# Issuing the first Q and the first K transfer of an attention kernel in two parts of 16 and 112 partitions

## The chip, the cores and the metric

The kernel runs on one core of a Trainium2 chip. A core has five engines that work side by side: TensorE (PE in the profile; its weight loads are listed as PEld), VectorE (DVE), ScalarE (ACT), GpSimd (POOL) and SyncE (SP), which here only issues transfers. Sixteen DMA engines move data between the chip's large memory (HBM) and the core's on-chip memory (SBUF, 128 partitions). The metric is the device time of one execution in microseconds (us).

## What is computed

For each of 8 x 12 = 96 heads, Q, K and V are 512 x 64 float32 arrays. The reference, cut to its core:

```
Q_norm = Q / (norm(Q, axis=-2) + 1e-10)        # norm over the 512 rows
K_norm = K / (norm(K, axis=-2) + 1e-10)
attn = einsum('bhnd,bhne->bhde', Q_norm, K_norm)       # 64 x 64 for each head
attn = exp(attn - max(attn)); attn = attn / (sum(attn) + 1e-10)
out = einsum('bhnd,bhde->bhne', V, attn)               # 512 x 64 for each head
```

Three inputs of 12.6 MB each are read once and one output of 12.6 MB is written once, so 50.3 MB of data pass through the DMA engines.

## The kernel before

Four heads make a unit `u` (HU = 4; 24 units), two units a step `s` (12 steps), two steps a group `w` (6 groups). A Q or K load of one unit fills 128 partitions with 4,096 bytes each (512 KB): 32 partitions a head, 16 rows of 64 numbers in each. In the middle of the program one load brings both units of a step (1,024 KB).

For every unit VectorE casts Q and K to bf16 side by side (`cast_qk`, line 213). TensorE multiplies this [Q|K] block with itself (`grams`, line 233), which gives the cross products K'Q and, on the diagonal, the squares from which the norms come. VectorE takes the diagonal (`squares`, line 240; `sums`, line 252), ScalarE makes the reciprocal norms (lines 258 and 259), GpSimd or VectorE scales (`scale_k`, line 263), TensorE transposes (`logits`, line 276), ScalarE takes the exponentials (line 282), VectorE normalises (line 291). V is loaded, cast (GpSimd, line 170, or VectorE, line 168), transposed on TensorE (line 302), copied back (line 166 or 168) and multiplied with the normalised matrix (`outs`, line 319). The result is copied from PSUM and stored (`store`, lines 204 to 207). Line 204 stores one result in three pieces of 92, 4 and 32 partitions.

The order of all this is laid down at build time by a planner, the class `Order`: each piece of work names engines with costs, what it comes after, and a rank. The planner plays the program through and hands back the order in which the pieces are emitted. Transfers are pieces of an engine called DMA, with at most `QUEUE = 8` in flight: in the program, too, an issue waits until the transfer eight places before it has landed.

The first four loads are not emitted where the planner has them, but ahead of everything else (the list `ahead`, line 462, and these lines):

```
    for r in range(2):
        load_qk(0, 0, r)
        load_qk(0, 1, r)
```

`load_qk(s, x, r)` loads Q (x = 0) or K (x = 1) of unit `2 * s + r`. For step 0, K goes through ScalarE's queue (line 181) and Q through SyncE's (line 187); all later loads go through SyncE's. The load named `HELD`, the K load of step 1's second unit, first lets VectorE write one number into its tile (line 179), and it and the loads behind it are emitted only after the piece `UNTIL`, the cast of unit 0's K. `UNTIL` and the first casts wait for the first loads to land.

The planner knows nothing of how a load is divided into transfers: its piece for a load is one transfer, before and after the change.

Of the kernel before, what the change touches and what calls it, by code (L numbers as in the profile page):

```python
# [102 lines left out]
def kernel(  # L103
# [7 lines left out]
    nc = tc.nc  # L111
# [15 lines left out]
    Qu = Q.rearrange("b h (p t) d -> (b h p) (t d)", t=T).rearrange("(w r e p) x -> w e p r x", r=2, e=2, p=128)  # L127
    Ku = K.rearrange("b h (p t) d -> (b h p) (t d)", t=T).rearrange("(w r e p) x -> w e p r x", r=2, e=2, p=128)
# [33 lines left out]
    qk32, v32, vb, qkb, gram, scr, kq, n2, r8, kqs, rq, lg, ex, ab, vps, vt, po, so = ({} for _ in range(18))  # L162
# [9 lines left out]
    def load_qk(s, x, r):  # L172

        w, e = divmod(s, 2)
        if s not in qk32:
            qk32[s] = qp.tile([128, 2, 2, T, D], F32, name="qk32")
        if HELD == ("l" + "qk"[x], s, r):

            nc.vector.memset(qk32[s][0:1, x, r, 0, 0:1], 0.0)
        if (s, x) == (0, 1):  # L180
            nc.scalar.dma_start(out=qk32[s][:, x, r].rearrange("p t d -> p (t d)"), in_=Ku[w, e, :, r])
        elif 2 * s + (r or 0) >= WIDE:
            nc.sync.dma_start(out=qk32[s][:, x, r].rearrange("p (m j) d -> p m (j d)", m=2), in_=(Qw, Kw)[x][U - 1])
        elif r is None:
            nc.sync.dma_start(out=qk32[s][:, x].rearrange("p r t d -> p r (t d)"), in_=(Qu, Ku)[x][w, e])
        else:
            nc.sync.dma_start(out=qk32[s][:, x, r].rearrange("p t d -> p (t d)"), in_=(Qu, Ku)[x][w, e, :, r])
# [143 lines left out]
# [3 lines that stand above are left out]
# [50 lines left out]
    for s in range(S):  # L384
        free = [back("cq", 2 * s + r, 2 * NB["qk"], x) for r in range(2) for x in range(2)]
        for r in parts(s):
            at = QK_PACE * (2 * s + (r or 0)) / U
            for x in range(2):
                key = loaded(x, s, r)
                piece(key, {"DMA": X if r is not None else 2 * X}, free, [last], at, load_qk, s, x, r)  # L390
                last = key
    for u in range(U):
        s, r = divmod(u, 2)
# [48 lines left out]
    for s in range(S):  # L442
        for x in range(4):
            i, k = divmod(x, 2)
# [59 lines left out]
```

## Time and profile before

The time before is 128.76 us, the median of three runs (128.62 to 128.79). The profile is of one execution. Its page gives the span from the first to the last instruction, 127.0 us; it does not list a time of that execution's own beside it. The median of the runs is 1.76 us longer than the span.

| | |
|---|---|
| median of three runs | 128.76 us |
| span of the profiled execution | 127.0 us |
| busy: TensorE, VectorE, ScalarE, GpSimd | 77.7, 92.8, 72.5, 36.6 us |
| moved by DMA | 50.64 MB, mean 399 GB/s over the span |
| mean granted TensorE clock | 0.832 |
| share of SyncE's DMA queue q1, of ScalarE's q10 | 96.4%, 2.1% |
| first Q and K issues begin | 0.74 and 0.73 us |
| first cast of Q begins | 5.39 us |
| last computing ends | 115.1 us |

How to read the lines that follow. In the strip of forty slices each digit is the busy share of a slice in tenths, 9 being 90% or more; the DMA row is the mean over the sixteen engines, and the row below gives GB/s. The same strip can be asked for a short window and then has slices of some ten nanoseconds. A packet is what one DMA engine moves at a time; the loads of Q and K use packets of 4,096 bytes, one for each partition. A packet counts in the slice in which it starts, with its whole duration, so a share in a very short window can be over 1. In a timeline a line gives start, duration, engine, source line, operation, tiles and count, and in brackets how long the engine had been idle and what released it; SPq and ACTq are the queues on which transfers are issued.

### The profile page before, as it was taken

The page shows a single profiled execution, that of the slowest core. Times are in us where ns is not written, and L with a number is a line of the kernel's source. Part 1 is how long each engine was busy: PE and PEld are TensorE (multiplying, and loading weights), DVE is VectorE, ACT ScalarE, POOL GpSimd, SP SyncE. Part 2 cuts the span into 40 slices and gives each one's busy share as a digit, 9 for nine tenths or more (in the row PEclk, how much of TensorE's full clock was granted, in tenths as well). Part 3 has the DMA queues.
Part 4 walks back from the last instruction along what each step waited for, and adds up shares of the span by engine and source line. Part 5 has one row for each costly group of instructions (what it writes and reads, how often), then busy time and mean ns, then how long its engine had stood idle before and what let it go on. Part 6 is the DMA issues. An engine that isn't in the chain of part 4 may idle for free.

```text
span 127.0 us, 4887 instructions
## 1 busy us (share of the span) xinstructions
PE 77.7 (61%) x2128; PEld 62.9 (50%) x2128; DVE 92.8 (73%) x141; ACT 72.5 (57%) x220; POOL 36.6 (29%) x40
## 2 busy tenths in 40 slices
PE   0065384894844679858594879566797869680000
PEld 0054372773633568647482668445585748460000
DVE  3354749859899899999885898999999799820000
ACT  4000441569877077786692786794829969972000
POOL 4006307300906903033065212213453361200000
PEclk9999999999998555999958967998559995955555
DMA  4999999999999999999999999999999999999993
GB/s 114 415 434 410 430 410 418 417 437 403 425 426 415 410 419 421 405 415 426 430 410 413 415 421 427 412 419 428 401 413 410 403 402 406 401 405 408 405 366 106
DMA packets 15629, 50.64 MB, mean 399 GB/s; under 512 B 1144, under 2 KB 1656, under 8 KB 14200
## 3 DMA queue, kind: packets, MB, share of 16 engines
q1 hardware_dynamic: 15320, 49.29, 96.4%
q10 hardware_dynamic: 288, 1.05, 2.1%
q8 instruction: 16, 0.26, 0.7%
q14 instruction: 5, 0.04, 0.1%
HBM read 37.75 MB, written 12.58 MB: 396 GB/s over the span
## 4 chain that ended last, share of the span: by engine, by line
DVE 39%; DMA 21%; PE 13%; ACT 11%; issue 4%; POOL 2%; DVEq 0%; SPq 0%; POOLq 0%; ACTq 0%
DMA qk<-in_Q_dram 21%; DVE qkb L213 15%; PE gram L233 9%; DVE scr L240 7%; DVE ab L291 6%; ACT vt L166 4%; DVE vb L168 4%; ACT ex L282 3%; ACT so L166 3%; PE vps L302 3%; DVE n L252 2%; DVE vt L168 2%; DVE so L168 2%; PE po L319 1%; ACT kq L166 1%
## 5 line engine op out<-in xcount | busy, mean ns | idle before, releaser
L233 PE MATMUL gram<-qkb 32*128 32x128 bf16 (+1 forms) x1504 | 35.5, 257 | 23.1 <-DVE qkb L213 9.9
L233 PEld LDWEIGHTS <-qkb 32*128 32x128 bf16 (+1 forms) x1504 | 29.9, 114 | 27.7 <-DVE qkb L213 12.7
L213 DVE CAST qkb<-qk 128x1024 bf16<-128x1024 f32 x48 | 36.4, 780 | 8.5 <-DMA qk<-in_Q_dram 6.9
L170 POOL TENSOR_SCALAR vb<-v 128x1024 bf16<-128x1024 f32 x19 | 21.2, 1129 | 45.5 <-DMA v<-in_V_dram 32.0
L166 ACT COPY so<-po 128x512 f32<-128x512 f32 x45 | 25.0, 593 | 5.2 <-PE po L319 5.0
L166 ACT COPY vt<-vps 128x1024 bf16<-128x1024 bf16 (+1 forms) x18 | 17.8, 989 | 17.4 <-PE vps L302 17.3
L302 PE MATMUL vps<-identb,vb 128*128 128x128 bf16 x192 | 20.2, 262 | 5.8 <-POOL vb L170 3.7
L319 PE MATMUL po<-ab,vt 128*64 128x128 bf16 x384 | 19.3, 242 | 5.2 <-issue 2.7
L263 POOL TENSOR_TENSOR kqs<-kq,r 64x512 f32<-64x512 f32 x12 | 14.0, 1164 | 25.8 <-ACT r L259 13.4
L240 DVE SCALAR_TENSOR_TENSOR scr<-gram,eye 64x512 f32<-64x512 f32 x24 | 16.5, 687 | 4.4 <-PE gram L233 4.1
L302 PEld LDWEIGHTS <-vb 128*128 128x128 bf16 x192 | 14.7, 117 | 10.0 <-POOL vb L170 5.1
L319 PEld LDWEIGHTS <-vt 128*64 128x64 bf16 x384 | 13.8, 121 | 9.2 <-issue 4.6
L282 ACT ACTIVATE ex<-lg,rq 128x64 f32<-128x64 f32 x48 | 14.5, 322 | 2.8 <-PE lg L276 2.7
L166 ACT COPY kq<-gram 64x512 f32<-64x512 f32 x12 | 7.0, 581 | 13.5 <-DVE scr L240 13.4
L291 DVE TENSOR_TENSOR ab<-ex,rinv 64x256 bf16<-64x256 f32 x24 | 13.9, 579 | 0.6
L282 ACT ACTIVATION_READ_ACCUMULATOR ex<-lg,rq 128x1 f32 x48 | 10.2, 213 | 0.0
L168 DVE CAST vb<-v 128x1024 bf16<-128x1024 f32 x5 | 7.6, 1527 | 1.2 <-DMA v<-in_V_dram 1.2
L252 DVE TENSOR_REDUCE n<-scr 128x8 f32<-128x512 f32 x12 | 8.1, 679 | 0.1
L276 PE MATMUL lg<-eye,kqs 64*128 64x64 f32 x48 | 6.4, 259 | 2.6 <-issue 1.5
L168 DVE COPY vt<-vps 128x1024 bf16<-128x1024 bf16 (+1 forms) x8 | 7.9, 1019 | 0.1
L276 PEld LDWEIGHTS lg<-eye,kqs 64*128 64x128 f32 x48 | 4.5, 156 | 4.4 <-issue 2.0
L288 DVE RECIPROCAL rinv<-esum 128x4 f32<-128x4 f32 x12 | 2.1, 171 | 2.8 <-ACT ex L282 2.8
(17 smaller groups left out, 16.0 us busy)
## 6 DMA issues: line engine op xcount, KB each, us to landing
v<-in_V_dram SPq DMA_DIRECT2D x11, 1024.0 KB, 17.1
out_dram<-so SPq DMA_DIRECT2D x22, 512.0 KB, 10.2
qk<-in_Q_dram SPq DMA_DIRECT2D x8, 1024.0 KB, 17.4
qk<-in_K_dram SPq DMA_DIRECT2D x8, 1024.0 KB, 17.1
qk<-in_Q_dram SPq DMA_DIRECT2D x8, 512.0 KB, 12.2
qk<-in_K_dram SPq DMA_DIRECT2D x6, 512.0 KB, 12.5
qk<-in_K_dram ACTq DMA_DIRECT2D x2, 512.0 KB, 7.3
v<-in_V_dram SPq DMA_DIRECT2D x2, 512.0 KB
```

Source lines behind the costliest of these rows:

```text
L166: nc.scalar.copy(o, i)
L168: nc.vector.tensor_copy(o, i)
L170: nc.gpsimd.tensor_scalar(out=o, in0=i, scalar1=1.0, scalar2=0.0, op0=ALU.mult, op1=ALU.add)
L213: nc.vector.tensor_copy(qkb[u][:, :, x * D:(x + 1) * D], qk32[s][:, x, r])
L233: nc.tensor.matmul(gram[s][:, h, r, 0], x, x, start=(t == 0), stop=(t == (T if u < WIDE else J) - 1))
L240: nc.vector.scalar_tensor_tensor(out=scr[s][half], in0=gram[s][half, :, :, 0, half].rearrange("p h r d -> p (h r) d"), scalar=1e-20, in1=e ...
L263: (nc.vector if eng == "DVE" else nc.gpsimd).tensor_tensor(out=kqs[s][HI], in0=kq[s][HI], in1=r8[s][HI, :, None].to_broadcast([D, 2 * HU, ...
L276: nc.tensor.transpose(l[:, h, :], kqs[s][HI, 2 * h:2 * h + 2].rearrange("p r d -> p (r d)"), eye2[HI])
L282: nc.scalar.activation(e[:, h, :], lg[s][:, h, :], AF.Exp, scale=rq[s][:, h:h + 1], accum_out=z[:, h:h + 1])
L291: nc.vector.tensor_tensor(out=a[half, :, half], in0=e[half], in1=ri[half, :, None].to_broadcast([D, HU, D]), op=ALU.mult,)
L302: nc.tensor.transpose(ps[:, c, n, :], vb[w][:, J * c + j].rearrange("p r d -> p (r d)"), identb)
L319: nc.tensor.matmul(po[s, x][e * D:(e + 1) * D, j].rearrange("p r d -> p (r d)"), v, ab[s][:, h, :])
```

## The change

For step 0, both Q and K now go through one branch. The loads of its second unit (r = 1) stay one transfer. The load of the first unit (r = 0) is issued as two transfers, one of partitions 0 to 15 (64 KB) and one of partitions 16 to 127 (448 KB), on the same queue as before: SyncE's for Q, ScalarE's for K. So SyncE issues one transfer more than before and ScalarE one more, and the first cast of each waits for two landings. Nothing else in the program is edited.

```
-        if (s, x) == (0, 1):
-            nc.scalar.dma_start(out=qk32[s][:, x, r].rearrange("p t d -> p (t d)"), in_=Ku[w, e, :, r])
+        if s == 0:
+            o, i = qk32[s][:, x, r].rearrange("p t d -> p (t d)"), (Qu, Ku)[x][w, e, :, r]
+            for rows in (slice(0, 16), slice(16, 128)) if r == 0 else (slice(None),):
+                (nc.sync, nc.scalar)[x].dma_start(out=o[rows], in_=i[rows])
         elif 2 * s + (r or 0) >= WIDE:
```

## The prediction

> **What bounds the kernel now.** I read the strip of forty slices first, then the DMA queues, then the first microseconds as a timeline, then the flow of the DMA engines in short windows at both ends. The strip of the page:
>
> ```profile
> DVE  3354749859899899999885898999999799820000
> DMA  4999999999999999999999999999999999999993
> GB/s 114 415 434 410 430 410 418 417 437 403 425 426 415 410 419 421 405 415 426 430 410 413 415 421 427 412 419 428 401 413 410 403 402 406 401 405 408 405 366 106
> DMA packets 15629, 50.64 MB, mean 399 GB/s; under 512 B 1144, under 2 KB 1656, under 8 KB 14200
> ```
>
> Each slice is 3.17 us. The DMA engines are full in every slice but the first and the last, at about 412 GB/s, while VectorE is free in the last four. The chain of waits gives VectorE 39% and DMA 21%, but it cannot say what a faster VectorE would meet: the engines that move the data have no hole to fill. So the program ends when 50.64 MB have passed, and it can end sooner only if the stream starts sooner, runs faster, or drains more evenly. Windows over the end say the same:
>
> ```profile
> 115.00:116.00 1.00, 0.00 (x0) 0.00 (x0) 0.00 (x0) 0.08 (x1) 0.00 (x0) 0.50 1.06 410
> 116.00:117.00 1.00, 0.00 (x0) 0.00 (x0) 0.00 (x0) 0.00 (x0) 0.00 (x0) 0.50 1.05 406
> 117.00:118.00 1.00, 0.00 (x0) 0.00 (x0) 0.00 (x0) 0.00 (x0) 0.00 (x0) 0.50 1.05 404
> 122.00:123.00 1.00, 0.00 (x0) 0.00 (x0) 0.00 (x0) 0.00 (x0) 0.00 (x0) 0.50 0.92 353
> 124.00:125.00 1.00, 0.00 (x0) 0.00 (x0) 0.00 (x0) 0.00 (x0) 0.00 (x0) 0.50 0.73 258
> ```
>
> The columns are the window, its length, busy time of PE, its weight loads, VectorE, ScalarE and GpSimd, the granted clock, the DMA share and GB/s. All computing is over at 115.1 us, and the stores still run at 400 GB/s for seven microseconds; then engines drop out one after another. Computing therefore has several microseconds of slack at the end, and a stream moved by x moves the end by x.
>
> The change lies at the start, whose timeline reads:
>
> ```profile
> 0.73 0.89 ACTq L181 DMA_DIRECT2D qk<-in_K_dram  x2
> 0.74 0.85 SPq L187 DMA_DIRECT2D qk<-in_Q_dram  x2
> 1.64 0.42 SPq L194 DMA_DIRECT2D v<-in_V_dram  x1
> 1.65 1.28 ACT L338 ACT_TABLE_LOAD   x1 [1.65 <-PEq L488]
> 5.39 1.29 DVE L213 CAST qkb<-qk 128x1024 bf16<-128x1024 f32 x2 [3.44 <-DMA qk<-in_Q_dram]
> ```
>
> Both queues begin to issue at 0.73 us. The DMA view cut to 1.6 to 2.3 us shows what came of it:
>
> ```profile
> GB/s 0 0 0 0 0 0 0 0 702 0 468 468 234 0 234 0 234 0 234 468 0 0 234 234 234 0 234 0 234 234 0 234 0 0 0 0 234 702 234 0
> DMA packets 25, 0.10 MB, mean 146 GB/s; under 512 B 0, under 2 KB 0, under 8 KB 25
> q1 hardware_dynamic: 25, 0.10, 66.8%
> ```
>
> A slice is 17.5 ns, and 234 GB/s is one packet of 4,096 B. The first packets start at 1.74 us, 1.0 us after the issue began, and the next come one by one; the sixteenth, one for each of the 16 engines, starts near 2.03. All are of SP's queue q1, the Q transfer. K's queue q10 has none, although ScalarE issued at the same moment; a view to 2.4 us holds its first five. So K's 128 rows come into the engines about 0.56 us behind Q's 128 rows, as if the rows of one transfer were prepared after those of the other, at some 0.56/128 = 4.4 ns a row (an estimate from these two starts). Windows of the ramp:
>
> ```profile
> 1.80:2.00 0.20, 0.00 (x0) 0.00 (x0) 0.15 (x1) 0.20 (x1) 0.20 (x1) 1.00 1.02 164
> 2.00:2.20 0.20, 0.00 (x0) 0.00 (x0) 0.00 (x0) 0.20 (x1) 0.03 (x1) 1.00 0.54 123
> 2.60:2.80 0.20, 0.00 (x0) 0.00 (x0) 0.00 (x0) 0.20 (x1) 0.00 (x0) 1.00 1.30 287
> 3.40:4.00 0.60, 0.00 (x0) 0.00 (x0) 0.00 (x0) 0.00 (x0) 0.00 (x0) 1.00 1.03 423
> ```
>
> At 412 GB/s the 0.56 us from 1.74 to 2.3 would hold 56 packets, and there were 25: 31 x 4,096 B / 412 GB/s = 0.31 us lost. From 2.3 to 3.3 us the view counts 77 packets where 100 fit: 0.23 us more. After that the stream is full. The whole ramp costs 0.54 us.
>
> **The change part by part.** The sum is made on the profiled execution's span, 127.0 us; the median of the three runs is 128.76, so 1.76 us lie outside the span, and I leave these alone.
>
> *The first transfer gets short.* Q's first issue carries 16 rows in place of 128. The trace has issues of few rows: the three stores of line 204, of 92, 4 and 32 partitions, took 0.26, 0.32 and 0.34 us (minimum, median, maximum), against 0.33 to 0.46 us for undisturbed issues of 128 rows at lines 181 and 187. The first packet should come earlier by that, 0.07 to 0.16 us; I take 0.10. If packets wait until all rows of their transfer are prepared, 112 fewer rows at 4.4 ns bring 0.49 us; if rows are handed over one by one, only the issue counts. The slow trickle between 1.74 and 2.03 speaks for handing over one by one, so I take the 0.10.
>
> *All engines begin together.* Sixteen packets on 16 engines would start within 16 x 4.4 ns = 0.07 us rather than over 0.29, if each engine gets one. K's 16 rows should follow at once, and two packets an engine (0.32 us at 0.159 us each, 4,096 B at a sixteenth of 412 GB/s; 0.8 us at the 0.41 us that the eight packets of the window from 1.8 to 2.0 took on average) keep the engines busy until the 112-row parts are there. Those are issued some 0.33 us behind the first parts. I take 0.20 of the 0.31 us; the bounds are none of it and 0.54, the whole ramp.
>
> *What it adds.* Two more transfers make 32 more 4-byte completion packets. The page has 1,144 such packets; two an engine cost 0.02 us by my estimate, since one-packet transfers of this kind leave no hole at 117 us. One more issue on SP (about 0.4 us) moves the V load from 1.64 to 2.0 and what follows on that queue by as much; the transfers before it hold 2.1 MB, five microseconds of flow, which covers it. One more issue on ScalarE moves the table load from 1.65 to about 2.05; ScalarE's first use is at 12.85, so it costs nothing while 9 us of cover stand. GpSimd's queue is not passed.
>
> *Waits.* There are eight transfers in flight (the planner's QUEUE), and a ninth issue waits for the first landing. With two more in front, the issues at 2.80 (K) and 3.37 us (Q) of the second pair come to be ninth and tenth and wait for the first parts, at worst for the landing of Q's 112 rows, until now 5.4 us. Behind them stand only loads that line 179's memset holds until 6.74 anyway. By then 3.7 MB are issued, which last until 2.3 + 8.9 = 11.2 us: cost nothing. From the eleventh on the eight-back partner is the same as now. The first cast waits for two landings instead of one; if it came 0.5 us later, the next cast, which waits for data until 7.98, would still be met (casts end at 6.68).
>
> Sum: -0.10 - 0.20 + 0.02 = -0.28 us; rounded with the stall of 2.6 to 2.8 us, which may shrink a little too, -0.3: 126.7 us of span, **128.45 us**. Bounds of this case: from about -0.05 (the issue alone, against the added packets) to -0.62 (issue and whole ramp).
>
> [...]
>
> **The rivals.** *Slower: the narrow parts write slowly.* Place: the sixteen packets per engine of the first Q and K. If a transfer of 16 or 112 rows lays several engines' writes on the same partitions, each packet takes longer than 0.159 us. Against it: the line 204 stores of 92, 4 and 32 partitions pass between 116 and 119 us, where the flow stays at 404 to 410 GB/s. But these read SBUF, and the change writes it. For it: packets in the ramp can be slow, 0.30 us on average in the window from 2.6 to 2.8 (share 1.30 x 0.2 us x 16 engines, over 14 packets). At a mean of 0.20 us the price is 16 x 0.041 = 0.66 us, less the 0.28 gained: +0.38, 129.1 us. It decides from 0.177 us a packet, where gain and loss meet.
>
> *No change: the slow start belongs to the first packets, not to the rows.* If the engines' first reads are slow whatever the transfer's size (0.41 us on average), the small part only takes the slow packets upon itself, and what the earlier issue brings is eaten by the second issue's delay. Time: 128.7, give or take 0.1. For it speaks that the DMA share is already 1.02 between 1.8 and 2.0: the engines count as busy, yet move 164 GB/s. The gap of 0.54 between 2.0 and 2.2 speaks against it.
>
> *The gain is lost behind.* If one engine that is late anyway sets the end, the mean gain need not reach it. The drain from 122 to 125.7 us shows such unequal engines. It would leave between nothing and 0.3; I count it within the two cases above.
>
> **How the numbers follow.** A measurement of this kernel tells changes of over 0.2%, 0.26 us, from none. Earlier start 0.55, of which about 0.10 falls inside 0.26 us, as its bounds reach from -0.05 to -0.62; narrow parts slow 0.28, for a load like this is simply not in the trace; no change 0.17. So faster 0.45, same 0.27, slower 0.28. The first case alone ranges from 128.15 to 128.7; the range for 8 in 10 is 128.1 to 129.1, leaving out the slow case's upper part.
>
> **What would show it.** Right: first packets before 1.70 us, packets of both queues by 2.0, well over 25 packets before 2.3, the full flow by 3.0, last stores issued about 0.3 us earlier than 119.6 and 120.0, and an unchanged 410 GB/s between. Wrong: flow under 300 GB/s until 4 us and a first cast well after 5.39 (narrow parts slow), or the same count of packets by 3.3 us (no change). A drop of the strip below 9 between slices 2 and 4 would mean that the moved waits starved the queue.

## The result and the profile after

The change makes the kernel slower: 129.56 us against 128.70 us, medians of five runs each; ratio 1.0065, 95% interval 1.0053 to 1.0077. That is 0.86 us lost, where 0.3 us of gain was forecast. The profiled execution took 129.49 us with a span of 127.7 us (before: 127.0).

The strip of forty slices after the change, DMA share and GB/s:

```profile
DMA  4999999999999999999999999999999999999993
GB/s 95 336 431 414 429 412 421 414 439 402 420 438 411 407 422 418 409 413 426 423 421 410 418 422 421 413 425 425 400 413 407 408 400 404 402 406 407 407 366 109
```

Before, the first two slices moved 114 and 415 GB/s; now they move 95 and 336. From the third on the two strips agree within some 15 GB/s, up and down. The missing bytes are (114 + 415 - 95 - 336) x 3.18 us = 312 KB, which take 0.76 us at 412 GB/s. So nearly all of the loss arises in the first 6.4 us, and the stream behind does not make it up. The digits of the DMA row are the same as before, 4 in the first slice and 9 in the second: the engines are as busy and move less.

The view of the DMA engines from 1.6 to 2.3 us after the change, in slices of 17.5 ns:

```profile
GB/s 0 0 0 0 0 0 0 0 0 468 936 234 0 0 0 0 0 0 0 0 0 0 468 234 234 702 234 234 0 0 0 0 235 937 235 702 235 703 234 234
DMA packets 46, 0.13 MB, mean 181 GB/s; under 512 B 15, under 2 KB 15, under 8 KB 46
q1 hardware_dynamic: 31, 0.07, 44.6%
q10 hardware_dynamic: 15, 0.06, 21.8%
```

The first packets start at 1.76 us, not earlier than before (1.74). Seven come together, then no packet starts for 0.19 us, then come the other nine of Q's sixteen, and right behind them, from 2.16 us on, K's (q10). The seven engines are not idle meanwhile: their packets took 0.41 us each (share 0.89 of 16 x 0.2 us in the first window below, over seven packets). Without the 15 completion packets of 4 bytes (the page after has 32 more packets under 512 B than the 1,144 before, sixteen for each added transfer), 31 packets have started by 2.3 us, where there were 25. Windows of the ramp after the change (columns as in the prediction: busy times of PE, its weight loads, VectorE, ScalarE and GpSimd, then clock, DMA share, GB/s):

```profile
1.60:1.80 0.20, 0.00 (x0) 0.00 (x0) 0.20 (x2) 0.00 (x0) 0.20 (x2) 1.00 0.89 143
1.80:2.00 0.20, 0.00 (x0) 0.00 (x0) 0.15 (x1) 0.00 (x0) 0.20 (x1) 1.00 0.07 20
2.00:2.20 0.20, 0.00 (x0) 0.00 (x0) 0.00 (x0) 0.06 (x1) 0.02 (x1) 1.00 0.82 266
2.60:2.80 0.20, 0.00 (x0) 0.00 (x0) 0.00 (x0) 0.20 (x1) 0.00 (x0) 1.00 1.22 184
2.80:3.00 0.20, 0.00 (x0) 0.00 (x0) 0.00 (x0) 0.20 (x1) 0.00 (x0) 1.00 0.71 143
3.40:4.00 0.60, 0.00 (x0) 0.00 (x0) 0.00 (x0) 0.02 (x1) 0.00 (x0) 1.00 0.92 300
4.00:5.00 1.00, 0.00 (x0) 0.00 (x0) 0.00 (x0) 0.00 (x0) 0.00 (x0) 1.00 1.02 352
5.00:6.00 1.00, 0.00 (x0) 0.00 (x0) 0.00 (x0) 0.00 (x0) 0.00 (x0) 1.00 1.04 328
```

and of the same two microseconds before the change:

```profile
4.00:5.00 1.00, 0.00 (x0) 0.00 (x0) 0.00 (x0) 0.00 (x0) 0.00 (x0) 1.00 1.02 414
5.00:6.00 1.00, 0.00 (x0) 0.00 (x0) 0.61 (x1) 0.00 (x0) 0.00 (x0) 1.00 1.02 397
```

At 2.4 us the changed kernel is slightly ahead (160 KB against 143 KB, summing the windows). Then it falls behind twice. From 2.4 to 3.4 us it moves 205, 184, 143, 184 and 328 GB/s where there were 246, 287, 287, 307 and 471: 111 KB, 0.27 us. The two queues from 2.3 to 3.3 us, before the change:

```profile
q1 hardware_dynamic: 39, 0.16, 51.1%
q10 hardware_dynamic: 38, 0.16, 44.9%
```

and after it:

```profile
q1 hardware_dynamic: 48, 0.19, 93.5%
q10 hardware_dynamic: 18, 0.01, 3.2%
```

Q's stream is there, but K's queue carries next to nothing: most of its 18 packets are completions, and K's 112 rows have hardly begun at 3.3 us, where K's full load had begun at 2.3. The second loss comes from 3.4 to 6 us, where the share is 0.92 to 1.04 and the flow 300 to 352 instead of 397 to 423 (205 KB, 0.50 us). As many busy engines move some five sixths of the bytes, so from 4 to 6 us a packet takes 0.19 to 0.21 us instead of 0.16. The timeline after the change:

```profile
0.73 1.38 ACTq L183 DMA_DIRECT2D qk<-in_K_dram  x3
0.74 1.33 SPq L183 DMA_DIRECT2D qk<-in_Q_dram  x3
2.11 0.43 SPq L196 DMA_DIRECT2D v<-in_V_dram  x1
6.12 1.29 DVE L215 CAST qkb<-qk 128x1024 bf16<-128x1024 f32 x2 [4.16 <-DMA qk<-in_Q_dram]
```

Three issues take 1.33 us where two took 0.85: an issue of 16 rows takes as long as one of 112 or 128 here (0.39 to 0.45 us each). The first casts begin at 6.12 us instead of 5.39, 0.73 us later, and the last group of stores is issued from 116.49 us on instead of 115.75, 0.74 us later. The shift made in the first six microseconds is carried through to the last stores.

### The profile page after: what moved, and what is told of

Read it like the earlier page. It is cut to its first block, busy times and chain, and to the rows that moved or that the text cites. A ratio compares the mean times of both kernels' runs of the same rounds, so it can differ in the third digit from the quotient of the medians.

```text
span 127.7 us, 4891 instructions
## 1 busy us (share of the span) xinstructions
PE 78.1 (61%) x2128; PEld 63.5 (50%) x2128; DVE 93.3 (73%) x141; ACT 72.6 (57%) x220; POOL 36.7 (29%) x40
## 4 chain that ended last, share of the span: by engine, by line
DVE 40%; DMA 22%; PE 16%; ACT 7%; issue 4%; ACTq 1%; DVEq 0%
DVE qkb L215 16%; DMA qk<-in_Q_dram 16%; PE gram L235 10%; DVE scr L242 7%; DVE ab L293 7%; DMA qk<-in_K_dram 6%; PE po L321 3%; DVE vb L168 3%; DVE n L254 3%; PE vps L304 3%; DVE vt L168 2%; ACT vt L166 2%; ACT ex L284 2%; ACT kq L166 1%; ACT so L166 1%
## 5 line engine op out<-in xcount | busy, mean ns | idle before, releaser
L235 PE MATMUL gram<-qkb 32*128 32x128 bf16 (+1 forms) x1504 | 36.7, 261 | 21.6 <-DVE qkb L215 7.5
L235 PEld LDWEIGHTS <-qkb 32*128 32x128 bf16 (+1 forms) x1504 | 31.1, 117 | 26.1 <-DVE qkb L215 10.0
L215 DVE CAST qkb<-qk 128x1024 bf16<-128x1024 f32 x48 | 36.9, 790 | 9.4 <-DMA qk<-in_Q_dram 7.7
L170 POOL TENSOR_SCALAR vb<-v 128x1024 bf16<-128x1024 f32 x19 | 21.8, 1157 | 43.6 <-DMA v<-in_V_dram 36.0
L321 PE MATMUL po<-ab,vt 128*64 128x128 bf16 x384 | 20.5, 247 | 6.4 <-issue 2.1
L265 POOL TENSOR_TENSOR kqs<-kq,r 64x512 f32<-64x512 f32 x12 | 13.5, 1129 | 28.4 <-ACT r L261 16.1
L304 PE MATMUL vps<-identb,vb 128*128 128x128 bf16 x192 | 18.0, 246 | 4.6 <-POOL vb L170 2.7
L321 PEld LDWEIGHTS <-vt 128*64 128x64 bf16 x384 | 14.5, 124 | 11.0 <-issue 5.9
L304 PEld LDWEIGHTS <-vb 128*128 128x128 bf16 x192 | 13.4, 109 | 7.9 <-POOL vb L170 3.6
```

Source lines behind the costliest of these rows:

```text
L170: nc.gpsimd.tensor_scalar(out=o, in0=i, scalar1=1.0, scalar2=0.0, op0=ALU.mult, op1=ALU.add)
L215: nc.vector.tensor_copy(qkb[u][:, :, x * D:(x + 1) * D], qk32[s][:, x, r])
L235: nc.tensor.matmul(gram[s][:, h, r, 0], x, x, start=(t == 0), stop=(t == (T if u < WIDE else J) - 1))
L265: (nc.vector if eng == "DVE" else nc.gpsimd).tensor_tensor(out=kqs[s][HI], in0=kq[s][HI], in1=r8[s][HI, :, None].to_broadcast([D, 2 * HU, ...
L304: nc.tensor.transpose(ps[:, c, n, :], vb[w][:, J * c + j].rearrange("p r d -> p (r d)"), identb)
L321: nc.tensor.matmul(po[s, x][e * D:(e + 1) * D, j].rearrange("p r d -> p (r d)"), v, ab[s][:, h, :])
```

## The experiments

Each run was timed beside the kernel before, whose median was 128.63 to 128.66 us; losses are against that. Besides the time, the bytes moved by 20 us are given where they bear on the argument (the DMA view cut to 0 to 20 us; before: 7.43 MB). They come from one execution of each kernel and show how far the stream is behind, without what happens at the end of the program.

**Tiny transfers in front.** Based on the kernel before:

```
     for i in range(2):
-        const.tile([128, D // 4], F32, name=f"front{i}")
+        f = const.tile([128, D // 4], F32, name=f"front{i}")
+        (nc.sync, nc.scalar)[i].dma_start(out=f[0:16], in_=(Qu, Ku)[i][0, 0, 0:16, 0, 0:D // 4])
```

> Q and K go whole, as before; ahead of them each queue issues one extra transfer of 16 partitions of 64 bytes into a tile that nobody reads. This has the two extra issues, the 32 extra completion packets and the shift of the eight-back waits, and none of the split. Theory A (the parts of the split tensors are laid badly over engines or partitions, so their packets take about 0.20 us instead of 0.16): 128.7 us, within 0.3 us of before. Theory B (the extra issues, completions and moved waits cost the time): 129.5 us, as after. Theory C (a small transfer at the head makes the ramp slow, whatever it carries): 129.3 us or more, with the flow below 300 GB/s until 4 us.

Measured: 129.32 us, ratio 1.0051 (1.0031 to 1.0070). Two transfers that carry next to nothing cost 0.66 us. The DMA view from 1.6 to 2.3 us of this kernel:

```profile
DMA packets 64, 0.00 MB, mean 3 GB/s; under 512 B 64, under 2 KB 64, under 8 KB 64
q10 hardware_dynamic: 32, 0.00, 2.5%
q1 hardware_dynamic: 32, 0.00, 2.4%
```

Until 2.3 us only the tiny packets and their completions have passed: the full loads stand behind one more issue and start some 0.55 us later. Theory A, that only the layout costs, is refuted as the whole story. Theory B, the extra issues, comes near the number; the next run that bears on it is the one with the same transfers behind the loads. Theory C's number is met too, but not its sign: the flow is 416 GB/s from 3.4 to 4.0 us.

**A split along the columns.** In the changed kernel:

```
-            for rows in (slice(0, 16), slice(16, 128)) if r == 0 else (slice(None),):
-                (nc.sync, nc.scalar)[x].dma_start(out=o[rows], in_=i[rows])
+            for cols in (slice(0, 128), slice(128, 1024)) if r == 0 else (slice(None),):
+                (nc.sync, nc.scalar)[x].dma_start(out=o[:, cols], in_=i[:, cols])
```

> The first Q and K are split along the columns: 128 partitions of 512 bytes, then 128 partitions of 3,584 bytes. As many transfers and as many bytes in each part as in the change, but all partitions in each part. Theory A: no packet of the second part is slowed, 128.4 to 129.0 us (the 256 small packets cost under 0.2 us). Theory B: 129.5 us. Theory C: 129.3 us or more.

Measured: 129.17 us, ratio 1.0038 (1.0025 to 1.0052). As many transfers and bytes as in the change, no narrow part: 0.51 us lost instead of 0.86. No theory had it; it lies between A and B. The windows in which the change has its second loss:

```profile
4.00:5.00 1.00, 0.00 (x0) 0.00 (x0) 0.00 (x0) 0.00 (x0) 0.00 (x0) 1.00 1.01 401
5.00:6.00 1.00, 0.00 (x0) 0.00 (x0) 0.24 (x1) 0.00 (x0) 0.00 (x0) 1.00 1.09 377
```

The flow is 401 and 377 GB/s where the change had 352 and 328. By 4 us both kernels are about equally late (0.56 MB here, 0.55 MB in the change, 0.72 MB before). So two costs are at work: a late start, which this run has too, and slow packets, which it has far less.

**Halves.** `(slice(0, 64), slice(64, 128))` in place of the 16 and 112 rows:

> Rows 0 to 63 and 64 to 127 instead of 16 and 112. Theory A: slow for the whole of the first Q and K; if it depends on how many groups of partitions a part reaches, at least as slow as after (129.5 us or more, up to 131). Theory B: 129.5 us, as after, since the transfers are as many. Theory C: about 128.7 us, since no part is small.

Measured: 131.04 us, ratio 1.0181 (1.0159 to 1.0204). The windows of this run:

```profile
4.00:5.00 1.00, 0.00 (x0) 0.00 (x0) 0.00 (x0) 0.00 (x0) 0.00 (x0) 1.00 1.02 217
5.00:6.00 1.00, 0.00 (x0) 0.00 (x0) 0.00 (x0) 0.00 (x0) 0.00 (x0) 1.00 1.04 221
```

The DMA share is full and the flow is just half of the usual 414. This is the slowness of a part that covers half of the partitions; but it is not all that this run loses. Its issues took 0.55 to 0.82 us each, no packet starts before 2.0 us, and at 4 us it has moved 0.46 MB where the kernel before had 0.72, so a part of the loss of 2.4 us is a late start.

**Every other row.** `(slice(0, 128, 2), slice(1, 128, 2))`:

> Even rows, then odd rows: 64 partitions in each part, spread over the whole of the on-chip memory. Theory A: clearly faster than the split in halves and near before (128.7 to 129.0 us), if it is the place of the partitions that matters, and like the halves if any part of fewer than 128 partitions is slow. Theory B: 129.5 us. Theory C: 128.7 us.

Measured: 130.95 us, median of six runs that scatter from 130.02 to 131.79, ratio 1.0170 (1.0134 to 1.0205). The flow was 320, 270 and 320 GB/s in the three microseconds from 4 us on, better than the halves' 217, 221 and 213, yet the time is no better within the scatter. The stream does tell the two apart: 6.82 MB by 20 us against the halves' 6.40, so 1.5 and 2.5 us behind. The expected 128.7 to 129.0 was missed by far: rows spread over the whole memory are slow too in this form, less than halves, and why is not shown.

**The tiny transfers behind the first four loads.** The same two transfers as in the first experiment, but after the loop that calls `load_qk(0, x, r)`:

> The same two extra transfers of 16 x 64 bytes, now issued behind the first four loads instead of ahead of them. Theory D (what stands ahead of the first full load delays it by its own issue, 0.45 us, and the stream with it; the rest is the layout of the parts): 128.7 us, within 0.25 of before, because full loads are already under way. Theory B (the extra completions and the moved eight-back waits cost the time): 129.3 us, as with the tiny transfers in front.

Measured: 128.94 us, ratio 1.0019 (1.0010 to 1.0027). The extra transfers, completions and moved waits together cost 0.29 us there, and 0.66 us in front. Theory D's bound of 0.25 was missed by a little; by the difference, more than half of the cost in front is the place. By 20 us this kernel has moved 7.38 MB, 0.12 us behind, and the tiny transfers in front 7.18 MB, 0.6 us behind.

**The large part first.** `(slice(0, 112), slice(112, 128))`:

> The same split with the large part first: rows 0 to 111, then rows 112 to 127. Theory D: the head loses nothing, the slow packets of the 112-row parts stay, 129.1 to 129.4 us, so 0.1 to 0.4 below after. If the head were all of it: 128.7 us. If a small part in front had even helped: 129.6 us or more.

Measured: 130.27 us, ratio 1.0125 (1.0111 to 1.0139), so 0.7 us worse than the change. Theory D and the theory of the head alone missed; the number lies where a small part in front had helped (129.6 or more). The windows show where:

```profile
5.00:6.00 1.00, 0.00 (x0) 0.00 (x0) 0.00 (x0) 0.00 (x0) 0.00 (x0) 1.00 1.08 230
6.00:7.00 1.00, 0.00 (x0) 0.00 (x0) 0.06 (x1) 0.00 (x0) 0.00 (x0) 1.00 0.96 238
```

The flow drops to 230 GB/s, where the change had 352 and 328 at its slow packets, at about the time when the 16-row parts come behind the large ones. In the running stream 16 rows are dear. At the head of the changed kernel they were not: K's 15 packets in its view from 1.6 to 2.3 us took 0.16 us each (21.8% of 16 x 0.7 us, over 15), like those of full loads.

**The split moved to the second unit.** `if r == 1` in place of `if r == 0`:

> The 16 and 112 split is taken from the first unit and put on the second one (r = 1), whose issues come when the stream runs. Theory D: the layout's part alone, 129.2 us (129.0 to 129.4), with the flow near 340 GB/s while those two loads pass, some two microseconds later than in after. If the loss belongs to the head alone: 128.7 us.

Measured: 130.84 us, ratio 1.0169 (1.0143 to 1.0196). The windows:

```profile
5.00:6.00 1.00, 0.00 (x0) 0.00 (x0) 0.01 (x1) 0.00 (x0) 0.00 (x0) 1.00 1.10 217
7.00:8.00 1.00, 0.66 (x28) 0.66 (x32) 0.28 (x2) 0.00 (x0) 0.00 (x0) 1.00 1.02 291
8.00:9.00 1.00, 1.00 (x48) 0.97 (x39) 0.00 (x0) 0.00 (x0) 0.00 (x0) 1.00 1.13 344
9.00:10.00 1.00, 0.24 (x12) 0.00 (x0) 0.00 (x0) 0.00 (x0) 0.00 (x0) 1.00 1.00 328
```

Two stretches: some two microseconds near 220 GB/s, then three at 291 to 344. By the order of issue the 16-row parts pass first and the 112-row parts behind them; but no completion packet comes between 6.2 and 8.5 us, so the 16-row parts are over by 6.2, and the rest of the first stretch belongs to the 112 rows. Against 420 GB/s the second stretch loses (129 + 76 + 92) KB, 0.71 us for two transfers; the first about 0.95 us. The price of the layout, which theory D had put at 0.5 us, was far too low once the parts stand in a full stream.

**Halves crossed.** `lo, hi` for Q and `hi, lo` for K:

> Halves again, but Q begins with rows 0 to 63 while K begins with rows 64 to 127, and then the other way round; everything else as in the halves run, which took 131.0 us. If the place of the partitions is what a part is short of (two parts in flight together reach all of them): well under the halves, 129.0 to 129.8 us, the flow above 300 GB/s from 3.4 to 7 us where the halves had 217. If any part of 64 rows is slow by itself: 131.0 us, as the halves.

Measured: 130.71 us, ratio 1.0172 (1.0147 to 1.0198): no better. But the run doesn't test what it was made for. In its DMA views from 2.0 to 3.2 us, and from 3.2 to 4.4 us, the two queues pass in turn:

```profile
q10 hardware_dynamic: 72, 0.25, 83.8%
q1 hardware_dynamic: 10, 0.04, 10.0%
```

```profile
q1 hardware_dynamic: 68, 0.22, 78.5%
q10 hardware_dynamic: 24, 0.07, 27.9%
```

K's half goes first, then Q's half; they were hardly ever in flight together, so no pair of them reached all partitions. It stays inconclusive.

**Q alone, K alone.** The condition `r == 0` becomes `(r, x) == (0, 0)` and `(r, x) == (0, 1)`:

> Only Q is split into 16 and 112; K goes whole on ScalarE's queue. Theory E (two costs: parts that do not cover all partitions move slowly, and a full load that stands behind an extra issue starts 0.45 us later): K's load keeps its place, so the head costs less than in after, and half the slow rows remain: 128.9 to 129.3 us. If the costs simply add by transfer: 129.1 us, half of the way to after.

> Only K is split; Q goes whole on SyncE's queue and so comes first into the engines. Theory E: 128.9 to 129.3 us, and together with the run that splits Q alone about the loss of after (0.8 to 0.9 us), or more, since now K's 16 rows pass behind full packets, as in the runs where they came later.

Measured: Q alone 128.94 us, ratio 1.0027 (1.0017 to 1.0037); K alone 129.40 us, ratio 1.0072 (1.0046 to 1.0097), 0.1 above its range. The sum of the two losses is 1.06 us, a little over the 0.86 of the change. With Q alone split, the view from 1.6 to 2.3 us has K's full load in it, which before came only at 2.3:

```profile
DMA packets 27, 0.11 MB, mean 152 GB/s; under 512 B 1, under 2 KB 1, under 8 KB 27
q1 hardware_dynamic: 17, 0.07, 41.2%
q10 hardware_dynamic: 10, 0.04, 40.3%
```

Up to 4.0 us this kernel moved 0.75 MB, where the kernel before moved 0.72 (the same view cut to 0 to 4 us): nearly 0.1 us ahead. A part of the gain that the forecast built on is there. Then Q's 112 rows pass, the flow falls to 340, 328 and 369 GB/s between 4 and 7 us, and more than the lead is lost (7.27 MB by 20 us, 0.4 us behind).

**Fewer issues; V first.** One transfer of both units for each queue, `(nc.sync, nc.scalar)[x].dma_start(out=qk32[0][:, x]..., in_=(Qu, Ku)[x][0, 0])`, and `load_v(0, 0, None)` ahead of the loop:

> The opposite of the change: for step 0 each queue issues one transfer of both units (128 partitions x 2 x 4,096 bytes) in place of two. If the slow ramp comes from the number of issues at the head: 128.2 to 128.5 us, faster than before. If the ramp is set by the first full load alone, which starts when it did: 128.65 us, as before; slower than 128.8 only if the later landing of the first unit is missed somewhere.

> The first V load (1,024 KB in packets of 8,192 bytes) is issued on SyncE's queue ahead of Q and K. If the slow ramp is a matter of rows (half as many per byte here): 128.3 to 128.5 us. If it is the first microsecond of any full load: 128.65 us. The casts begin 1 to 2 us later, which is covered unless the end moves as well.

Measured: joined 128.63 us, ratio 1.0001 (0.9992 to 1.0009); V first 128.82 us, ratio 1.0015 (1.0007 to 1.0024). Neither fewer issues nor longer rows shorten the ramp. With V first the flow was 307 GB/s from 1.6 to 2.0 us, and then no packet starts until 2.4; the first ones took 0.95 us each (share 2.23 of 16 x 0.4 us, over 15 packets of 8,192 bytes). Both kernels are in fact behind at 20 us, with 7.31 and 7.28 MB, 0.29 and 0.36 us, and show none or half of it in their time. In the joined run the lag lasts until the end of full flow (49.58 MB by 122 us against 49.69) and then halves (50.56 by 125 us against 50.61), while the engines run out of work one after another. So a small shift of the stream need not reach the end.

**64 KB more, in three forms.** Based on the kernel before, behind the first four loads:

```
+    spare = const.tile([128, 4, T * D], F32, name="spare")
+    for i in range(4):
+        nc.sync.dma_start(out=spare[0:16, i], in_=Qu[0, 0, 0:16, 0])
```

with `0:128:8` for the rows in the second form and `spare[0:128, i, 0:128]`, `Qu[0, 0, 0:128, 0, 0:128]` in the third.

> Before, with four extra transfers of 64 KB behind the first four loads, each of partitions 0 to 15 (4,096 bytes), into a tile nobody reads. The bytes alone are 0.16 us each, 0.63 us in all. If neighbouring partitions are slow to write (the flow halves, as where the 16-row parts stood in the running stream): about 0.45 to 0.6 us each, 130.5 to 131.0 us. If only the bytes count: 129.3 us.

> The same four extra transfers, each of 16 partitions eight apart (0, 8, ... 120). If the place matters: clearly cheaper than neighbours, 129.3 to 130.0 us. If 16 partitions are slow wherever they are: as with neighbours, 130.5 to 131.0 us.

> The same four extra transfers of 64 KB, each of 128 partitions of 512 bytes. All partitions, small packets: 129.3 to 129.6 us (0.63 us of bytes, and up to 0.3 us for 512 packets). This is the price of bytes and of four more transfers without narrow parts.

Measured: neighbours 131.47 us, ratio 1.0221 (1.0199 to 1.0243), 0.71 us for each transfer; eight apart 129.90 us, ratio 1.0099 (1.0082 to 1.0117), 0.32 us for each; 128 partitions of 512 bytes 130.92 us, ratio 1.0178 (1.0160 to 1.0197), 0.57 us for each. The bytes alone are 0.16 us. The second is in its range, the first 0.5 us above it, and the third, put at 129.3 to 129.6, missed by far. Windows from 8 to 9 us of the three, in this order:

```profile
8.00:9.00 1.00, 0.75 (x29) 0.48 (x20) 0.31 (x1) 0.00 (x0) 0.00 (x0) 1.00 1.56 176
```

```profile
8.00:9.00 1.00, 0.69 (x28) 0.42 (x16) 0.59 (x1) 0.00 (x0) 0.00 (x0) 1.00 1.05 262
```

```profile
8.00:9.00 1.00, 0.77 (x32) 0.50 (x20) 0.85 (x2) 0.00 (x0) 0.00 (x0) 1.00 0.61 130
```

The first pair settles that the place of the rows counts. The same number of rows, of the same size, 16 neighbours or 16 spread out: the neighbours cost more than twice as much, with the engines' packets overlong (share 1.56 at 176 GB/s). In all these runs the rows in HBM change along with the partitions (16 neighbours are 64 KB in one piece, those eight apart lie 32 KB from one another), so no run separates the reading side from the writing side. The measured prices also hold whatever any extra transfer costs there (0.29 us for two tiny ones): 0.16 us of bytes with half of that make 0.30 us, nearly the whole 0.32 of the rows eight apart. What makes the neighbours dearer is not shown. The third form is slow in another way: its share is 0.61, so the engines have holes.

**Only Q by columns.** The split by columns under `if (r, x) == (0, 0)`:

> Only the first Q is split, by columns: 128 partitions of 512 bytes, then of 3,584 bytes; K goes whole. If the early entry of K's full load is a gain by itself: the stream is 0.05 to 0.15 us ahead at 4 us and stays there, 128.5 to 128.6 us. If the extra issue takes it back: 128.65 to 128.8 us.

Measured: 128.61 us, ratio 1.0000 (0.9989 to 1.0011). One more issue in front of Q alone costs no time that could be measured when no row is slow. The stream was not ahead, though: 0.62 MB by 4 us against 0.72 before, and 7.36 MB by 20 us, 0.17 us behind. So the first expectation is met in its number but not in its reason, and this is a third run whose lag the end does not show. Against it, the same split of Q by rows lost 0.30 us. No version beat the kernel before.

## Why the prediction was wrong, step by step

The bound was read rightly: the stream of DMA sets the end, and in this change the shift at the start reached the last group of stores whole (0.73 us at the first cast, 0.74 at those stores). "A stream moved by x moves the end by x" is too strong as a rule: in the joined, the V-first and the Q-by-columns runs the stream was 0.29, 0.36 and 0.17 us behind, and the time 0, 0.18 and 0 longer. The prediction's third rival, "the gain is lost behind", had this in mind for a gain.

Wrong was the sign of the shift. The step that failed is the pair "All engines begin together", -0.20, and "What it adds", +0.02: the small parts were to keep the engines busy until the 112-row parts came, and the extra issue was to cost almost nothing. In their place stands a late start: 0.23 us by 3.4 us in the windows (0.27 less the 0.04 that it was ahead), or 0.51 us by the columns split. On top came slow packets while the 112-row parts pass, which the sum left out and a rival had: 0.50 us by the windows from 3.4 to 6 us, or 0.35 us by the difference of the change and the columns split. The two ways of counting don't agree on which cost is the larger, and the columns split has small packets that may cost something of their own; so both costs are shown, and their shares are not.

- *"The first transfer gets short", -0.10.* It does not. The issues of 16 rows took 0.39 to 0.45 us, as long as those of 128 rows, and the first packet came at 1.76 instead of 1.74. The stores of line 204, from which the step was priced, stand on a queue late in the program; they were the wrong row. The first packet came 1.0 us after the issue began, for 16 rows as for 128 and for 64 bytes a row as for 4,096; in the joined run it came at 1.9 us, and in the runs with 64 rows a part, whose issues took longer, after 2.0.
- *"All engines begin together", -0.20.* They did not: seven packets, then nine 0.2 us later. K's packets come in sooner, and at 2.4 us the changed kernel is 17 KB ahead: 0.04 us. With Q alone split the lead was nearly 0.1 us at 4 us. The estimate behind the step, 4.4 ns to prepare each row, would put K's first packet 0.07 us behind Q's when 16 rows are ahead of it. With the tiny transfers the seventeenth of their 32 packets had started by 1.95 us, so K's first came at most 0.21 us behind Q's at 1.74; but in the changed kernel, also with 16 rows ahead, it came 0.40 us behind (2.16 against 1.76). So the number of rows alone does not set it; that Q's bytes ahead on the same engines do is the likely reading, and not tested.
- *"What it adds", +0.02.* Two extra transfers cost 0.29 us behind the first loads and 0.66 us in front. The 112 rows, nearly all of the first load, stand behind one more issue of 0.4 us. The prediction had named this delay, at 0.33 us, and let the 128 KB of the small parts fill it; they take 0.31 us at full flow, and K's large part had hardly begun at 3.3 us.
- *"Waits", nothing.* In the changed kernel this holds: the strip stays at 9 from the second slice to the last but one.
- *The rivals.* "The narrow parts write slowly" came nearest: it priced a mean of 0.20 us a packet, and from 4 to 6 us the flow of 352 and 328 GB/s at full share is 0.19 to 0.21 us a packet. Its sum of +0.38 still had the gain of 0.28 in it, which did not come; without that gain it had 0.66, more than the 0.35 to 0.50 measured, and it knew nothing of the late start. The evidence against it, the narrow stores of line 204 at 404 to 410 GB/s, was the wrong neighbour: those stores read the on-chip memory. "No change" had named the second issue's delay, and took it to eat the gain and no more.

What the 16 rows cost depended on where they stood. At the head K's packets took 0.16 us each, as in full loads. In the running stream such a part costs 0.71 us, 0.55 above its bytes, so 1.1 us for two. What was slow in the change was the time of the 112-row parts (0.19 to 0.21 us a packet from 4 to 6 us); why is not shown.

## What to carry to other kernels

When a kernel is bound by its transfers, leave the first full load at the front of its queue: here it reached the engines 1.0 us after its issue, and a transfer of 64 bytes a row ahead of it on each of two queues cost 0.66 us, against 0.29 behind the loads. A transfer that fills only some neighbouring partitions is slow per byte (0.71 us for 64 KB to 16 neighbours, 0.32 to 16 spread out, 0.16 if it flowed fully). Spreading alone does not make a split cheap: even and odd rows lost 2.3 us. By columns the same loads lost less than by rows (0.51 against 0.86 us for Q and K, nothing measurable against 0.30 for Q alone). A split must be priced in a row that moves data in the same direction: the narrow stores of line 204 passed at 404 to 410 GB/s, the 112-row loads at 328 to 352. And look at the bytes moved as well as at the time: where the engines run dry one after another at the end, the time hid lags of up to 0.3 us.

## What was not expected of the hardware

The 64 KB transfers of 128 rows of 512 bytes cost 0.57 us each in the running stream, nearly as much as 16 neighbouring rows, and with the engines idle for more than a third of the time (share 0.61). At the head of Q's queue the same shape cost no measurable time (128.61 us). Why the engines stand idle there was not followed up.

The ramp resists: with a column split, one joined transfer or V first, the engines take until 3.2 to 3.6 us to flow fully. After the first packets none starts for 0.2 us or more (20 GB/s from 1.8 to 2.0 us after the change, nothing from 2.0 to 2.4 with V first), while the first ones, 0.41 and 0.95 us long, are still under way. Why the first packets take so long stays open.
